# A transformer block with 32 routed experts: expert blocks 128 or 96 slots wide, and an adding DMA that skips empty slots

## The chip, the core and the metric

The kernel runs on one core of a Trainium2 chip. The metric is the device time of one execution in microseconds (us). A core has a matrix engine (PE, whose weight loads the profile lists apart as PEld), a vector engine (DVE), a scalar engine (ACT), a general engine (POOL) and a sync engine (SP), and 16 DMA engines that move data between the memory and the core's buffers.

## The reference, cut to what matters

The block takes 1024 tokens of width 1024. A dilated attention and a recurrent branch come first, then a projection, a norm and a router that gives every token the two best experts of one group of eight. The change lies in the last part, the experts:

```python
# per token: 2 experts of 32, each with a gate value
def expert_block(args):                       # xb: tokens of one expert, e: the expert
    xb, e = args
    hid = jax.nn.silu(xb @ w_expert_gate[e]) * (xb @ w_expert_up[e])   # 1024 -> 512
    return hid @ w_expert_down[e]                                      # 512 -> 1024
yb = lax.map(expert_block, (xin, blk_expert)).reshape(n_rows, D)
y = jax.ops.segment_sum(yb * row_gate[:, None], row_tok, num_segments=T + 1)[:T]
```

The result is added to the residual stream. All is float32. Weights are 6 MB an expert, 201 MB for the 32.

## The kernel before

Everything before 1159 us of the profile (projection, recurrent scan, attention, mixing, router) is the same in both kernels. From there the kernel runs one block per expert. A block has `CAP = 96` slots; an expert with more tokens has the rest done in a loop behind the blocks, which does not run for this data.

The token numbers of an expert stand in a column of the table `tbl`, one slot in a partition; a slot without a token holds a number past the last row (`1 << 20` and more). An indirect DMA from POOL (`gather`, L1504) brings the 96 rows into `xin`, a tile of 128 partitions by 1024; it has a bound, and rows past it are skipped, so that the 32 partitions above and the empty slots hold zeros or old rows.

float32 products are made of halves: each operand is split into a rounded part ("hi") and the rest ("lo"), and three matmuls stand for one: hi by hi, lo by hi, hi by lo. For the tokens, `xpose` transposes `xin` on PE (L1525, against `ident`) into a PSUM tile, four pieces at a time; ACT writes the hi half from it (L1526), DVE the lo half (L1527). The halves of the input are `xTh` and `xTl` (8 pieces, so two evictions each per expert), those of the hidden rows `hTh` and `hTl` (4 pieces, one each).

The weights of an expert come in 12 chunks of 512 KB (8 for gate and up, 4 for down) by SP's queue. Each is split: ACT makes hi (L1415), and lo is made by DVE for about ten chunks and by POOL for two (every sixth; the last 30 chunks all go to DVE), both L1417. The halves go into nine pairs of buffers `u`.

In `acc` (L1531) the token halves are stationary and 512 columns of the weights move. Gate and up are 48 matmuls into two PSUM tiles `pb`; ACT applies Silu to one (L1584), and DVE multiplies the other onto it (L1585), which gives `hd`. Down is 24 matmuls into two tiles `pa`, evicted with the gate value by DVE (L1605) and ACT (L1606) into `row`. Then `add_rows` (L1510) adds the rows to the output by an indirect DMA that POOL issues. It has no bound here: the output has 128 rows of padding, and the table `tba`, made by four small DVE instructions, points each empty slot at its own padding row.

The steps run (gate/up of expert e), (down of expert e-1), with the transposes of the next tokens and of the hidden rows put among the matmuls (`xpose_hi`). In which order each engine gets its instructions is decided when the program is built, by a scheduler that goes by its own estimate of each instruction's cost; `xpose_hi` gives the transposes and their evictions a higher priority.

Here a POOL or DVE "split" means the L1417 instruction (128x1024 in, 128x1024 out), "add" the instruction of L1510 and "gather" that of L1504.

Of the kernel before, what the change touches and what calls it, by code (L numbers as in the profile page):

```python
# [10 lines left out]
F32 = mybir.dt.float32  # L11
F32R = mybir.dt.float32r
BF = mybir.dt.bfloat16
I32 = mybir.dt.int32
U32 = mybir.dt.uint32
AF = mybir.ActivationFunctionType
ALU = mybir.AluOpType
# [4 lines left out]
S = 1024  # L22
# [16 lines left out]
CAP = 96  # L39
# [143 lines left out]
def block_kernel(ctx, tc, I, out, dbg=None):  # L183
    nc = tc.nc
# [31 lines left out]
    ident = cst.tile([128, 128], F32, name="ident")  # L216
# [64 lines left out]
    def pb(shape):  # L281
        return psB.tile([128] + shape, F32, name="pb")
# [38 lines left out]
    for k in range(8):  # L321
# [4 lines left out]
        if k == 7:  # L326
# [3 lines left out]
                                       op0=ALU.mult, op1=ALU.subtract)  # L330
        for i in range(2):
            for kk in ([k] if i == 0 or k > 1 else [] if k == 0 else [0, 1]):
                for h in range(2):
                    hs = slice(h * 512, (h + 1) * 512)
                    for n, (a, b) in enumerate(((0, xhi), (0, xlo), (1, xhi))):
                        nc.tensor.matmul(ps0[i][h], w0[i][a][:, kk, :], b[:, kk, hs],
                                         start=(kk == 0 and n == 0), stop=(kk == 7 and n == 2))
    for h in range(2):
        hs = slice(h * 512, (h + 1) * 512)
        for k in range(8):  # L340
            for n, (a, b) in enumerate(((0, xhi), (0, xlo), (1, xhi))):
                nc.tensor.matmul(ps0[2][h], w0[2][a][:, k, :], b[:, k, hs], start=(k == 0 and n == 0),
                                 stop=(k == 7 and n == 2))
# [12 lines left out]
    for h in range(2):  # L356
        pt = psB.tile([128, 4, 128], F32, name="pb")
# [52 lines left out]

# [1 line left out]
    hrs = [slice(0, 64), slice(64, 128)]  # L412
# [28 lines left out]
    pT = sT.enter_context(tc.tile_pool(name="pT", bufs=1, reuse_waits="tile"))  # L441
# [37 lines left out]
    for p in range(4):  # L479
        cs = slice(128 * p, 128 * p + 128)  # L480
        for h in range(2):
            hs = slice(h * 512, (h + 1) * 512)
            ps = pb([512])
# [6 lines left out]
            nc.gpsimd.dma_start(dGG[p][:, hs], gt)  # L490
# [1 line left out]
    tab = p1.tile([32, 12], F32, name="tab", bufs=1)  # L492
# [5 lines left out]
    for g in range(3):  # L498
        pt = psB.tile([128, 384], F32, name="pb")
# [45 lines left out]
    def prep(p):  # L545
# [18 lines left out]
        for h in range(2):  # L564
# [13 lines left out]
            for j in range(4):  # L578
                nc.tensor.matmul(pn[:, 2 * j:2 * j + 2], kks[:, j * 128:(j + 1) * 128], cc("ind2"),
                                 start=True, stop=True)  # L580
# [54 lines left out]
            tstep()  # L635
            # token-major copies
            BT = p1.tile([128, 4, 2, 128], F32, name="BT")
# [9 lines left out]
            tstep()  # L647
            # chunk-local products
            pbn = pb([512])
# [114 lines left out]
    if MP & 2 and not MP & 1:  # L764
        mp.enter_context(tc.manual_schedule(engines={mybir.EngineType.PE}))
# [1 line left out]
    s2 = ExitStack()  # L767
# [110 lines left out]

# [1 line left out]
    s3 = ExitStack()  # L880
# [211 lines left out]

# [1 line left out]
    pmx = s9.enter_context(tc.tile_pool(name="pmx", bufs=2, reuse_waits="tile"))  # L1094
# [57 lines left out]

# [1 line left out]
    def gate(gi, n, h, ga=None):  # L1154
# [62 lines left out]

# [1 line left out]
    def route(i, pl, r2):  # L1219
# [272 lines left out]
    rstep()  # L1492
    # slots without a token point past the last row
    gr = cst.tile([128, 64], F32, name="gr")
# [5 lines left out]

# [1 line left out]
    def gather(dst, src, idx):  # L1502
# [5 lines left out]
    def add_rows(src, idx):  # L1508
        src = src[0:idx.shape[0]]
        nc.gpsimd.indirect_dma_start(out=out, out_offset=bass.IndirectOffsetOnAxis(ap=idx, axis=0),  # L1510
                                     in_=src, in_offset=None, compute_op=ALU.add)

# [5 lines left out]
    def xpose(src, kt, name):  # L1518
        hi = pm.tile([128, kt, 128], F32R, name=name + "h")
        lo = pm.tile([128, kt, 128], F32R, name=name + "l")  # L1520
        sv = src.rearrange("q (p k) -> q k p", k=kt)
        for q in range(kt // 4):
            pt = pb([4, 128])
            for j in range(4):
                nc.tensor.transpose(pt[:, j], sv[:, 4 * q + j], ident)  # L1525
            nc.scalar.activation(hi[:, 4 * q:4 * q + 4], pt, AF.Copy)  # L1526
            nc.vector.tensor_tensor(lo[:, 4 * q:4 * q + 4], pt, hi[:, 4 * q:4 * q + 4].bitcast(F32), op=ALU.subtract)  # L1527
        return hi, lo

    def acc(ps, w, x, first, last):  # L1530
        nc.tensor.matmul(ps, x, w, start=first, stop=last)  # L1531

# [16 lines left out]
    tailm.close()  # L1549
    tpad = pm.tile([128, 2], F32, name="tpad")  # L1550
    nc.vector.tensor_scalar(tpad[:, 0:1], tokid[:, 0:1], float(S), None, op0=ALU.add)
    nc.vector.tensor_scalar(tpad[:, 1:2], tpad[:, 0:1], -1.0, float(1 << 20), op0=ALU.mult, op1=ALU.add)
    tba = pm.tile([128, 32], I32, name="tba")
    tocc = pm.tile([128, 32], F32, name="tocc")
    nc.vector.tensor_scalar(tocc, pT[:, 96:128], tpad[:, 1:2], tpad[:, 0:1], op0=ALU.mult, op1=ALU.add)
    nc.vector.tensor_tensor(tba, tocc, pT[:, 0:32], op=ALU.add)

# [4 lines left out]
    for m, e in steps:  # L1562
        if m == 0:
# [19 lines left out]
            hd = pm.tile([128, 512], F32, name="hd", bufs=2)  # L1583
            nc.scalar.activation(hd, pg_, AF.Silu, scale=rsl[:, e:e + 1])  # L1584
            nc.vector.scalar_tensor_tensor(hd, pu_, rsl[:, e:e + 1], hd, op0=ALU.mult, op1=ALU.mult)  # L1585
            hid[e] = hd
            if e == N_EXP - 1:
                hT = xpose_hi(hid.pop(e), 4, "hT")
        else:
# [14 lines left out]
            rw = row if e < N_EXP - 2 else xin[e % 2]  # L1604
            nc.vector.tensor_scalar(rw[:, 0:512], pd[0], gat[:, e:e + 1], None, op0=ALU.mult)  # L1605
            nc.scalar.activation(rw[:, 512:1024], pd[1], AF.Copy, scale=gat[:, e:e + 1])  # L1606
            add_rows(rw, tba[0:CAP, e:e + 1])
    s9.close()

    sm.close()  # L1610
# [1 line left out]
    dTBv = dTB.rearrange("(q e) w -> q e w", e=32)  # L1612
# [89 lines left out]
```

## Time and profile before

| what | us |
|---|---|
| median of three executions (1787.35, 1787.5, 1788.68) | 1787.5 |
| span of the profiled execution | 1787.2 |
| expert stage within it, from the first gate/up matmuls | 1159 to 1776 |
| busy over the whole span: PE, DVE, ACT, POOL | 1680.3, 1263.4, 873.7, 461.6 |

The span is the time between the first and the last instruction of the profiled execution; the execution's own time lies 0.3 us above it, which is the median. The busy share of PE over the whole says little on the expert stage, where DVE is busy nearly all the time; the stage has to be read by its own windows. In rows of the timeline the first number is the start, the second the duration, and a bracket gives the idle time before it and what ended that. A `x3` joins three neighbours into one row.

### The profile page before, as it was taken

How to read it: one execution, taken by the hardware profiler on the slowest of the kernel's cores; microseconds unless marked ns; L12 is line 12 of the kernel's file. 1: busy time of each engine (PE TensorE's matmuls, PEld its weight loads, DVE VectorE, ACT ScalarE, POOL GpSimd, SP SyncE). 2: the span in 40 equal slices, each digit the busy share in tenths (PEclk: the TensorE clock that was granted, in tenths of full speed). 3: DMA queues.
4: the chain of work that ended last, by engine and by line, in shares of the span. 5: the costliest groups of instructions: out<-in, count | busy, mean ns of one | idle time of the engine just before them, and what ended most of it. 6: DMA issues, size and time to landing. Idle time of an engine off the chain costs nothing. (4 is left out here: it accounts for less than half of the span.)

```text
span 1787.2 us, 25862 instructions
## 1 busy us (share of the span) xinstructions
PE 1680.3 (94%) x9395; PEld 1325.3 (74%) x9396; DVE 1263.4 (71%) x2122; ACT 873.7 (49%) x1315; POOL 461.6 (26%) x380
## 2 busy tenths in 40 slices
PE   8999999999999999999998999699998999899996
PEld 6677777777777777777766777588777877777884
DVE  5647788783664444444436666689999999999985
ACT  4523434422221333344342122388777888777774
POOL 0110112223431000000100311234455455444431
PEclk9998989998999999999999999799999999999998
DMA  8323223363662110111249773699999999999991
GB/s 285 138 69 133 92 92 116 136 241 119 219 198 80 33 45 30 48 40 51 101 145 259 220 288 130 220 307 362 358 349 309 378 343 382 356 354 360 373 348 28
DMA packets 145619, 363.44 MB, mean 203 GB/s; under 512 B 17316, under 2 KB 62772, under 8 KB 145484
## 3 DMA queue, kind: packets, MB, share of 16 engines
q1 hardware_dynamic: 123108, 303.67, 47.4%
q0 software_dynamic: 15872, 50.35, 10.1%
q10 hardware_dynamic: 6504, 7.69, 1.6%
q8 instruction: 76, 1.25, 0.3%
q14 instruction: 59, 0.48, 0.1%
HBM read 307.49 MB, written 62.29 MB: 207 GB/s over the span
## 5 line engine op out<-in xcount | busy, mean ns | idle before, releaser
L1531 PE MATMUL pb<-u,xTh 128*128 128x512 f32 x1024 | 338.4, 406 | 1.2 <-ACT xTh L1526 1.2
L307 PE MATMUL pa<-xlo,wh 128*128 128x512 f32 x736 | 307.7, 418 | 0.0
L307 PE MATMUL pa<-xhi,wl 128*128 128x512 f32 x736 | 302.1, 411 | 2.3 <-DVE wl L278 2.3
L307 PE MATMUL pa<-xhi,wh 128*128 128x512 f32 x736 | 301.7, 410 | 1.5 <-DVE raw L427 1.0
L1417 DVE TENSOR_TENSOR u<-raw,u 128x1024 fp32r<-128x1024 f32 x182 | 297.5, 1676 | 5.5 <-ACT u L1415 5.3
L1415 ACT ACTIVATE u<-raw 128x1024 fp32r<-128x1024 f32 x216 | 224.3, 1056 | 47.5 <-PE pb L1531 28.8
L1531 PE MATMUL pb<-u,xTl 128*128 128x512 f32 x512 | 209.2, 409 | 21.1 <-DVE xTl L1527 21.1
L1531 PEld LDWEIGHTS pb<-u,xTh 128*128 128x128 f32 x1024 | 191.3, 189 | 40.7 <-ACT xTh L1526 2.0
L307 PEld LDWEIGHTS pa<-xlo,wh 128*128 128x128 f32 x736 | 141.1, 192 | 40.6 <-issue 11.0
L307 PEld LDWEIGHTS pa<-xhi,wh 128*128 128x128 f32 x736 | 141.4, 192 | 34.5 <-issue 2.9
L307 PEld LDWEIGHTS pa<-xhi,wl 128*128 128x128 f32 x736 | 141.6, 192 | 34.1 <-DVE wl L278 3.2
L1417 DVE TENSOR_TENSOR u<-mix,u 128x1024 fp32r<-128x1024 f32 x108 | 162.2, 1538 | 4.4 <-ACT u L1415 4.4
L1531 PE MATMUL pa<-u,hTh 128*128 128x512 f32 x512 | 146.0, 406 | 5.5 <-POOL u L1417 4.6
L1415 ACT ACTIVATE u<-mix 128x1024 fp32r<-128x1024 f32 x128 | 133.6, 1057 | 23.1 <-PE pb L1531 15.8
L1531 PEld LDWEIGHTS pb<-u,xTl 128*128 128x128 f32 x512 | 96.8, 189 | 45.0 <-DVE xTl L1527 27.9
L978 DVE SCALAR_TENSOR_TENSOR Sb<-pb,rqk,bias 128x128 f32<-128x128 f32 (+1 forms) x96 | 35.5, 406 | 124.5 <-PE pb L977 116.6
L1510 POOL DMA_INDIRECT out<-row,tba x30 | 62.6, 2086 | 219.4 <-ACT u L1415 56.5
L1531 PEld LDWEIGHTS pa<-u,hTh 128*128 128x128 f32 x512 | 94.6, 191 | 28.2 <-POOL u L1417 5.5
L1417 POOL TENSOR_TENSOR u<-raw,u 128x1024 fp32r<-128x1024 f32 x34 | 101.3, 2980 | 47.2 <-ACT u L1415 41.6
L276 ACT ACTIVATE wh<-wr 128x1024 fp32r<-128x1024 f32 x49 | 51.8, 1057 | 113.9 <-PE pa L307 90.1
L1531 PE MATMUL pa<-u,hTl 128*128 128x512 f32 x256 | 81.6, 400 | 1.2 <-DVE hTl L1527 1.2
L982 ACT ACTIVATE Sb<-Sb,ML 128x128 f32<-128x128 f32 (+1 forms) x96 | 42.3, 442 | 54.7 <-DVE ML L980 54.7
(419 smaller groups left out, 3014.4 us busy)
## 6 DMA issues: line engine op xcount, KB each, us to landing
raw<-in_w_expert_up SPq DMA_DIRECT2D x72, 512.0 KB
raw<-in_w_expert_gate SPq DMA_DIRECT2D x71, 512.0 KB
raw<-in_w_expert_down SPq DMA_DIRECT2D x71, 512.0 KB
wr<-in_w_in SPq DMA_DIRECT2D x49, 512.0 KB
mix<-in_w_expert_down SPq DMA_DIRECT2D x46, 512.0 KB
mix<-in_w_expert_gate SPq DMA_DIRECT2D x42, 512.0 KB
mix<-in_w_expert_up SPq DMA_DIRECT2D x40, 512.0 KB
dGA<-gs POOLq DMA_DIRECT2D x32, 256.0 KB, 3.6
```

What stands on the lines that cost most here:

```text
L276: nc.scalar.activation(wh, wr, AF.Copy)
L307: nc.tensor.matmul(ps, a[:, k, :], b[:, k, hs], start=(n == 0), stop=(n == 23))
L978: nc.vector.scalar_tensor_tensor(Sb[:, hh, 0:nk], pS[:, 0:nk], u.rn[:, 0, i, hh:hh + 1], u.bias[:, hh, 256 - nk:], op0=ALU.mult, op1=ALU.add)
L982: nc.scalar.activation(Sb[:, hh, 0:nk], Sb[:, hh, 0:nk], AF.Exp, bias=u.ML[:, i, hh:hh + 1], accum_out=u.ML[:, i, 2 + hh:3 + hh])
L1415: nc.scalar.activation(hi, raw, AF.Copy)
L1417: en.tensor_tensor(lo, raw, hi.bitcast(F32), op=ALU.subtract)
L1510: nc.gpsimd.indirect_dma_start(out=out, out_offset=bass.IndirectOffsetOnAxis(ap=idx, axis=0), in_=src, in_offset=None, compute_op=ALU.add)
L1531: nc.tensor.matmul(ps, x, w, start=first, stop=last)
```

## The change

The expert blocks become 96 wide all through: the transposes take 96 rows and give 96 columns, the halves `xT` and `hT` are 8 and 4 pieces of 96 columns, the matmuls have 96 stationary columns and 96 result rows, and the evictions, Silu and the multiplication work on 96 partitions. The adding DMA takes `tbl` and a bound, as the gather does, so that empty slots are skipped; the four DVE instructions that made `tba` go. The padding rows of the output stay allocated, and nothing adds to them any more in the blocks.

```diff
     def add_rows(src, idx):
         src = src[0:idx.shape[0]]
         nc.gpsimd.indirect_dma_start(out=out, out_offset=bass.IndirectOffsetOnAxis(ap=idx, axis=0),
-                                     in_=src, in_offset=None, compute_op=ALU.add)
+                                     in_=src, in_offset=None, bounds_check=S - 1, oob_is_err=False, compute_op=ALU.add)
...
     def xpose(src, kt, name):
-        hi = pm.tile([128, kt, 128], F32R, name=name + "h")
-        lo = pm.tile([128, kt, 128], F32R, name=name + "l")
+        hi = pm.tile([128, kt, CAP], F32R, name=name + "h")
+        lo = pm.tile([128, kt, CAP], F32R, name=name + "l")
         sv = src.rearrange("q (p k) -> q k p", k=kt)
         for q in range(kt // 4):
-            pt = pb([4, 128])
+            pt = pb([4, CAP])
             for j in range(4):
-                nc.tensor.transpose(pt[:, j], sv[:, 4 * q + j], ident)
+                nc.tensor.transpose(pt[:, j], sv[0:CAP, 4 * q + j], ident[0:CAP, 0:CAP])
...
-        nc.tensor.matmul(ps, x, w, start=first, stop=last)
+        nc.tensor.matmul(ps[0:CAP], x, w, start=first, stop=last)
...
-    tpad = pm.tile([128, 2], F32, name="tpad")
-    nc.vector.tensor_scalar(tpad[:, 0:1], tokid[:, 0:1], float(S), None, op0=ALU.add)
-    nc.vector.tensor_scalar(tpad[:, 1:2], tpad[:, 0:1], -1.0, float(1 << 20), op0=ALU.mult, op1=ALU.add)
-    tba = pm.tile([128, 32], I32, name="tba")
-    tocc = pm.tile([128, 32], F32, name="tocc")
-    nc.vector.tensor_scalar(tocc, pT[:, 96:128], tpad[:, 1:2], tpad[:, 0:1], op0=ALU.mult, op1=ALU.add)
-    nc.vector.tensor_tensor(tba, tocc, pT[:, 0:32], op=ALU.add)
...
-            nc.scalar.activation(hd, pg_, AF.Silu, scale=rsl[:, e:e + 1])
-            nc.vector.scalar_tensor_tensor(hd, pu_, rsl[:, e:e + 1], hd, op0=ALU.mult, op1=ALU.mult)
+            hc, rc_ = hd[0:CAP], rsl[0:CAP, e:e + 1]
+            nc.scalar.activation(hc, pg_[0:CAP], AF.Silu, scale=rc_)
+            nc.vector.scalar_tensor_tensor(hc, pu_[0:CAP], rc_, hc, op0=ALU.mult, op1=ALU.mult)
...
-            nc.vector.tensor_scalar(rw[:, 0:512], pd[0], gat[:, e:e + 1], None, op0=ALU.mult)
-            nc.scalar.activation(rw[:, 512:1024], pd[1], AF.Copy, scale=gat[:, e:e + 1])
-            add_rows(rw, tba[0:CAP, e:e + 1])
+            gc = gat[0:CAP, e:e + 1]
+            nc.vector.tensor_scalar(rw[0:CAP, 0:512], pd[0][0:CAP], gc, None, op0=ALU.mult)
+            nc.scalar.activation(rw[0:CAP, 512:1024], pd[1][0:CAP], AF.Copy, scale=gc)
+            add_rows(rw, tbl[0:CAP, e:e + 1])
```

The changed sizes change the scheduler's estimates, and with them the order. Up to about the 18th expert every engine's order is the same as before; from there on it differs at several places.

POOL from the 18th add on, before (`row` is the evicted block, `u` a weight half, `xin` the gathered tokens):

```order
L1510 DMA out<-row,tba 1152x1024
L1417 TENSOR_TENSOR u<-mix,u 128x1024
L1417 TENSOR_TENSOR u<-raw_12892,u 128x1024
L1504 DMA xin_9920<-dH_77,tbl 96x1024
L1510 DMA out<-row,tba 1152x1024
```

The same place after the change:

```order
L1510 DMA out<-row,tbl 1152x1024
L1417 TENSOR_TENSOR u<-mix,u 128x1024
L1504 DMA xin_9920<-dH_77,tbl 96x1024
L1417 TENSOR_TENSOR u<-raw_12917,u 128x1024
L1510 DMA out<-row,tbl 1152x1024
```

The gather has moved from behind POOL's second split to ahead of it; between an add and the next there are still two splits and one gather.

DVE from the 21st `hd` on, before:

```order
L1585 SCALAR_TENSOR_TENSOR hd<-pb,gr,hd 128x512
L1527 TENSOR_TENSOR xTl<-pb,xTh 128x512
L1417 TENSOR_TENSOR u<-mix,u 128x1024
L1527 TENSOR_TENSOR xTl<-pb,xTh 128x512
L1417 TENSOR_TENSOR u<-mix,u 128x1024 x3
L1605 TENSOR_SCALAR row<-pa,gr 128x512
L1417 TENSOR_TENSOR u<-mix,u 128x1024
L1527 TENSOR_TENSOR hTl<-pb,hTh 128x512
```

The same place after:

```order
L1579 SCALAR_TENSOR_TENSOR hd<-pb,gr,hd 96x512
L1527 TENSOR_TENSOR xTl<-pb,xTh 128x384
L1417 TENSOR_TENSOR u<-mix,u 128x1024
L1600 TENSOR_SCALAR row<-pa,gr 96x512
L1417 TENSOR_TENSOR u<-mix,u 128x1024 x3
L1527 TENSOR_TENSOR hTl<-pb,hTh 128x384
```

The second `xTl` no longer stands behind `hd`: at these experts one of the two is made ahead of `hd`, between the splits. The multiplication and the row eviction have 96 partitions and the same 512 columns; the three lo evictions have 384 columns for 512.

PE at the end of an expert's gate/up part some experts later, just ahead of its first down matmuls (`pa`), before:

```order
L1531 MATMUL pb<-u,xTh 128x512
L1525 MATMUL pb<-ident,xin_9920 128x128
L1531 MATMUL pb<-u,xTl 128x512
L1525 MATMUL pb<-ident,xin_9920 128x128
L1531 MATMUL pb<-u,xTh 128x512
L1525 MATMUL pb<-ident,xin_9920 128x128
L1531 MATMUL pb<-u,xTh 128x512
L1531 MATMUL pb<-u,xTl 128x512
L1525 MATMUL pb<-ident,xin_9920 128x128 x4
L1531 MATMUL pa<-u,hTh 128x512 x4
```

The corresponding stretch after:

```order
L1531 MATMUL pb<-u,xTh 96x512
L1525 MATMUL pb<-ident,xin_9920 128x96 x4
L1531 MATMUL pb<-u,xTh 96x512
L1531 MATMUL pb<-u,xTl 96x512
L1531 MATMUL pb<-u,xTh 96x512 x2
L1531 MATMUL pb<-u,xTl 96x512
L1531 MATMUL pb<-u,xTh 96x512
L1525 MATMUL pb<-ident,xin_9920 128x96 x2
```

The eight transposes of the next tokens have moved from the very end of the gate/up part to its middle, in fours and twos; the number of matmuls is the same.

## The prediction, made before the changed kernel ran

> **What bounds the kernel now.** I read the page's busy rows and slices first, for where the changed part lies, then busy time by windows in the expert stage, then PE's own timeline and waits there, then one period of DVE and POOL. Of the page (the slices are fortieths of the span):
>
> ```profile
> span 1787.2 us, 25862 instructions
> PE 1680.3 (94%) x9395; PEld 1325.3 (74%) x9396; DVE 1263.4 (71%) x2122; ACT 873.7 (49%) x1315; POOL 461.6 (26%) x380
> DVE  5647788783664444444436666689999999999985
> ```
>
> DVE's 71% hides a stage: in the last third it is at nine tenths or more. Two windows of the expert stage (columns: window, length, PE, PEld, DVE, ACT, POOL busy, granted clock, DMA share, GB/s):
>
> ```profile
> 1284.88:1364.12 79.24, 73.07 (x336) 59.75 (x336) 79.24 (x62) 61.69 (x70) 37.31 (x16) 1.00 0.99 351
> 1651.10:1705.10 54.00, 54.00 (x256) 45.11 (x254) 49.70 (x44) 40.40 (x49) 26.98 (x12) 1.00 1.03 372
> ```
>
> In the first, four experts long, DVE has no idle moment and PE has; in the second, three experts, PE has none and DVE has. So the stage has two limits close together. PE's first down matmuls of some experts give their sizes:
>
> ```profile
> 1186.16 0.48 PE L1531 MATMUL pa<-u,hTh 128*128 128x512 f32 x1
> ...
> 1493.34 0.95 PE L1531 MATMUL pa<-u,hTh 128*128 128x512 f32 x3
> ...
> 1513.08 1.18 PE L1531 MATMUL pa<-u,hTh 128*128 128x512 f32 x4
> ...
> 1651.15 1.18 PE L1531 MATMUL pa<-u,hTh 128*128 128x512 f32 x4
> 1669.13 0.72 PE L1531 MATMUL pa<-u,hTh 128*128 128x512 f32 x2
> ...
> 1741.15 0.71 PE L1531 MATMUL pa<-u,hTh 128*128 128x512 f32 x2
> ```
>
> 1513.08 - 1493.34 = 19.74 us an expert where DVE sets the pace, 1669.13 - 1651.15 = 17.98 where PE does. From 1186.16 to 1741.15 there are 29 periods in 555.0 us; at 17.98 they would take 521.4. All that this change can give without making PE's own work shorter is thus 33.6 us. What PE waits for there:
>
> ```profile
> PE pb L1531 <- DVE xTl L1527: 21.1, 15, 1.6
> PE pa L1531 <- POOL u L1417: 4.6, 2, 2.8
> 1518.77 0.63 PE L1531 MATMUL pb<-u,xTh 128*128 128x512 f32 x2
> 1520.93 0.50 PE L1531 MATMUL pb<-u,xTl 128*128 128x512 f32 x1 [1.54 <-DVE xTl L1527]
> ```
>
> The 15 waits for the lo half of the tokens stand once per slow expert. DVE is late as a whole, and this is where PE finds out. One DVE period, from one `hd` to the next, and POOL beside it:
>
> ```profile
> 1499.72 0.74 DVE L1585 SCALAR_TENSOR_TENSOR hd<-pb,gr,hd 128x512 f32<-128x512 f32 x1
> 1500.39 0.67 DVE L1527 TENSOR_TENSOR xTl<-pb,xTh 128x512 fp32r<-128x512 f32 x1
> ...
> 1506.12 0.73 DVE L1605 TENSOR_SCALAR row<-pa,gr 128x512 f32<-128x512 f32 x1
> 1506.78 1.21 DVE L1417 TENSOR_TENSOR u<-raw,u 128x1024 fp32r<-128x1024 f32 x1
> 1507.92 0.67 DVE L1527 TENSOR_TENSOR hTl<-pb,hTh 128x512 fp32r<-128x512 f32 x1
> 1508.52 4.34 DVE L1417 TENSOR_TENSOR u<-raw,u 128x1024 fp32r<-128x1024 f32 x1
> 1512.78 4.57 DVE L1417 TENSOR_TENSOR u<-raw,u 128x1024 fp32r<-128x1024 f32 x2
> ...
> 1519.54 0.74 DVE L1585 SCALAR_TENSOR_TENSOR hd<-pb,gr,hd 128x512 f32<-128x512 f32 x1
> 1507.66 1.66 POOL L1510 DMA_INDIRECT out<-row,tba  x1 [9.26 <-DMA mxh<-in_w_expert_down]
> 1508.85 2.92 POOL L1417 TENSOR_TENSOR u<-raw,u 128x1024 fp32r<-128x1024 f32 x1
> 1512.85 3.42 POOL L1417 TENSOR_TENSOR u<-mix,u 128x1024 fp32r<-128x1024 f32 x1 [1.08 <-ACT u L1415]
> ```
>
> Start to start, a split that nothing holds up costs 1.13 (1506.78 to 1507.92), an eviction 0.60 (1507.92 to 1508.52), `hd` and `row` 0.66 each (1506.12 to 1506.78). By the code ten splits, three lo evictions and the two others stand in a period: 11.35 + 1.80 + 1.33 = 14.48. The period is 19.82. The missing 5.34 stands in two splits: the one at 1508.52 takes 4.26 until the next start instead of 1.13 (3.13 more), and among the two at 1512.78 one has 3.43 instead of 1.21 (2.22 more). Both run while POOL runs a split of its own, and each ends 1.09 after POOL's does (1512.86 against 1511.77). DVE therefore stands still behind POOL's splits for over a quarter of the period.
>
> **The narrower lo evictions.** DVE's time goes by columns. Two rows that differ in columns only:
>
> ```profile
> L1225 DVE SCALAR_TENSOR_TENSOR lg<-pb,r,br x8: 240/242/244, 1038.8 to 1143.2; 128x32 f32<-128x32 f32 x8
> L1527 DVE TENSOR_TENSOR hTl<-pb,hTh x32: 672/676/692, 1177.7 to 1769.3; 128x512 fp32r<-128x512 f32 x32
> ```
>
> (676 - 242) / 480 = 0.904 ns a column, so 384 columns for 512 save 0.115 us an eviction, 0.345 an expert. `hd` and `row` keep 512 columns and lose only partitions: nothing. How much of the 0.345 counts? `hTl` stands just ahead of the first blocked split. That split's end hangs on POOL's, and POOL's on the add, which is issued on `row`, before `hTl`. So a shorter `hTl` only makes the split begin to wait earlier: I count 0.23, with 0.345 as the other end. In the first 19 experts the order is unchanged, and PE stands 19 x 0.23 = 4.4 us less (6.6 at the other end).
>
> **The new order from expert 19.** Before, an add is followed by two splits of POOL and then the gather; now by a split, the gather, a split. The trace has this order already in its fast stretch:
>
> ```profile
> 1654.01 2.42 POOL L1417 TENSOR_TENSOR u<-raw,u 128x1024 fp32r<-128x1024 f32 x1 [1.05 <-ACT u L1415]
> 1654.41 3.11 DVE L1417 TENSOR_TENSOR u<-raw,u 128x1024 fp32r<-128x1024 f32 x1
> 1657.44 0.68 DVE L1527 TENSOR_TENSOR xTl<-pb,xTh 128x512 fp32r<-128x512 f32 x1
> 1662.70 4.56 DVE L1417 TENSOR_TENSOR u<-raw,u 128x1024 fp32r<-128x1024 f32 x2
> 1667.19 3.48 DVE L1417 TENSOR_TENSOR u<-mix,u 128x1024 fp32r<-128x1024 f32 x3
> ```
>
> There the blocked splits lose 3.03 - 1.13 = 1.90 and 4.49 - 2.27 = 2.22, together 4.12 for 5.34, since POOL's split no longer stands in line behind the add's descriptors. With the 0.345, DVE's sum becomes 14.48 - 0.345 + 4.12 = 18.25. Experts 19 to 23 took 98.4 us before (19.8 each, the last 19.1); at 18.25 they take 91.3: 7.1 less. The second `xTl` that now comes ahead of `hd` moves no work, it only makes the wait at 1520.93 come later, on `hd` or a split; I give it nothing. Experts 24 to 28 already stand on PE's 17.98: nothing.
>
> **PE.** 72 matmuls and 12 transposes an expert stay. The matmuls move 512 columns as before; I take 17.98 as it is. The weight loads get narrower, 96 columns for 128, but they lie under the matmuls:
>
> ```profile
> L1531 PEld LDWEIGHTS pb<-u,xTh x1024: 186/188/333, 1159.0 to 1765.4; 128*128 128x128 f32 x171
> L1003 PEld LDWEIGHTS pb<-PT,Vt x280: 132/136/138, 600.4 to 919.8; 128*64 128x64 f32 x140
> ```
>
> By these, 96 columns take about 162 ns, 26 less than 188, under a matmul step of 230 ns (the rows of the first down matmuls: three take 0.95, four 1.18). Between nothing and 72 x 0.026 = 1.9 us an expert I take nothing, the row of the fast window being PE busy without a gap. The Trainium skill, "TensorE: Matmul & The Clock Gate", section "LDWEIGHTS (loading the stationary operand)", has the load grow with the columns at P / 1.2 ns, 107 for 128, and the trace has 188; by its slope the same 27 ns would go, so the sum would not differ by it.
>
> **The add.** Its DMA traffic falls: empty slots move nothing. That traffic is on no path: SP's loads wait for buffers, not the engines for loads.
>
> ```profile
> SPq L1320 <- DVE u L1417: 195.0, 175, 3.4
> L1510 POOL DMA_INDIRECT out<-row,tba x30: 1637/1660/6590, 1194.9 to 1749.1; - x30
> L1504 POOL DMA_INDIRECT xin<-dH,tbl x32: 965/1802/1902, 1149.8 to 1705.6; - x32
> ```
>
> No loads come sooner for it, since what a load waits for is the split that frees `raw`. The bound could change the add's time on POOL. The nearest row is the gather, which has a bound and as many rows: 0.965 at least, 1.802 in the middle, against 1.637 and 1.660. An add that lets POOL's split begin sooner or later moves DVE by as much, so the ends are -0.67 and +0.14 an expert, over some 24 experts -16 and +3.4. I take nothing: it is the same instruction on the same 96 slots, and the gather's two durations differ by what DVE does beside it, not by the bound. The longest add, 6.59, is a stray one; PE's two waits for POOL's split, 4.6 together, are what such an add leaves behind. It may come or go, and is kept.
>
> **Start and tail.** The four small DVE instructions go (about 0.1 to 0.2 us each, beside the first matmuls), the first and last evictions are shorter and stand on the path: together I put 0.5, an estimate.
>
> Sum: -4.4 - 7.1 - 0.5 = -12.0 on the profiled execution's 1787.2, with 0.3 around it (it stands at the median, 1787.5): **1775.5 us**.
>
> **Rivals.**
> (a) *DVE slips in front of POOL.* Which of the two splits holds the other hangs on a few tenths: DVE's split starts 0.33 ahead of POOL's (1508.52 against 1508.85) and is blocked all the same. With `hTl` 0.115 shorter it starts 0.45 ahead. If that is enough to keep it running, only POOL's later work meets DVE: a period of 14.48 - 0.345 + 2.22 + 1.90 (POOL's delayed split against the next of DVE's, taken as in the fast stretch) = 18.25 from the start. Over some 24 slow experts 24 x 0.27 = 6.5 of the 33.6 us stay: 1760, and 1754 if nothing stays. Against it: the start, 1508.52, lies inside the add (1507.66 to 1509.32), and 0.115 sooner still does; it would have to slip in ahead of what the add leaves for POOL to do, not of the split alone.
> (b) *Nothing is passed on.* Each blocked split is tied to POOL, so shorter evictions before either of the two are eaten, the new order loses to new collisions or to a stray add of 6.6 us more: 1785, between 1781 and 1789.
> (c) *96 is another geometry (slower).* PE changes between the transposes, which have 96 rows, and the matmuls, with 96 columns:
>
> ```profile
> 437.81 0.86 PE L865 MATMUL pb<-UVs,MCs 128*64 128x64 f32 x12
> 438.60 0.50 PE L307 MATMUL pa<-xlo,wh 128*128 128x512 f32 x1
> ```
>
> In the first row 12 matmuls take 0.06 apart and the next geometry begins about 0.15 after the last: 0.09 us a change. With some 16 changes an expert, 1.4 us, PE's floor becomes 19.4, and 31 experts take about 1793. It decides from 0.1 us a change on, where PE overtakes DVE's 19.6. The Trainium skill, "TensorEngine Tiling (Array Packing)", section "Key Properties", says that changing the tiling mode drains the engine; its section "Tiling Modes" knows 128, 64 and 32 only, by which 96 stays in the full array and costs nothing. No run here shows 96.
> (d) *The load counts.* If the matmul step does follow the load, PE's floor falls by up to 1.9 us. That is seen only where DVE has time left, 49.70 of 54.00 for three experts, so 1.4 us for each of the last five: 7 more, 1768.
>
> **Chances.** My forecast 0.52, with a range of its own of 1768 to 1782 (an add shorter by half of 0.67 in the first 19; nothing from the new order); (a) 0.20; (b) 0.16; (c) 0.07; (d) 0.05. The range from 1755 to 1788 takes in (a) but for its best end, (d), and (b) but for its worst end, and leaves out (c): under 2 in 10 together. A measurement of this kernel tells 0.2%, 3.6 us, from no change: faster takes the forecast, (a), (d) and a little of (b), 0.80; same is most of (b), 0.12; slower is (c) and the worst of (b), 0.08.
>
> **What would show it.** Right: in the profile after, the lo evictions of L1527 at 0.56 us; PE at 17.98 in the fast stretch; the period of the early experts near 19.6 with both blocked splits still there; experts 19 to 23 near 18.3; PE's waits for `xTl` down from 21.1 to some 10. Wrong: a period near 18.2 from the start (a); `xTl` waits unchanged (b); PE's fast stretch longer than 17.98 (c) or shorter (d); an add that is not 1.66.

## The result, and the profile after

The changed kernel took 1768.2 us, median of 11 executions (1752.47 to 1776.86), against 1788.68 for the kernel before (11 executions, 1778.11 to 1801.95): a ratio of 0.9871, 95% interval 0.9842 to 0.9899. The forecast was 1775.5. The profiled execution is one of the quickest, 1754.57 with a span of 1752.7:

```profile
span 1752.7 us, 25894 instructions
PE 1662.1 (95%) x9395; PEld 1253.9 (72%) x9396; DVE 1208.9 (69%) x2118; ACT 853.5 (49%) x1315; POOL 504.3 (29%) x380
```

The two spans can't be set against each other as they stand. In all profiles of this study the work ahead of the expert stage ended anywhere from 1142.8 to 1172.6 us, though its instructions are the same but for a few that zero a tile in some of the runs. One such place, before and then after (the column behind the brackets is the granted clock):

```profile
400.00:430.00 30.00, 28.38 (x360) 22.93 (x359) 11.19 (x21) 7.45 (x12) 9.98 (x16) 0.72 0.31 103
```

```profile
400.00:430.00 30.00, 27.44 (x470) 21.99 (x468) 11.15 (x21) 9.81 (x17) 12.22 (x20) 1.00 0.36 115
```

In the execution with the lower clock, 360 matmuls ran in these 30 us where the other ran 470. So I compare the expert stage alone, from its first gate/up matmul to the end, and split it at the first down matmuls of the experts, which PE's timeline shows. For the changed kernel:

```profile
1172.82 0.68 PE L1531 MATMUL pa<-u,hTh 128*96 128x512 f32 x2
...
1512.89 0.68 PE L1531 MATMUL pa<-u,hTh 128*96 128x512 f32 x2
...
1605.41 0.40 PE L1531 MATMUL pa<-u,hTh 128*96 128x512 f32 x1
...
1706.62 0.64 PE L1531 MATMUL pa<-u,hTh 128*96 128x512 f32 x2
```

Their distances, worked out in the same way for all kernels (us; "start" is the first gate/up matmul, "stage" runs from there to the end of the span; 29 experts lie between the first and the last boundary):

| kernel | start | experts 0-18 | 19-23 | 24-28 | stage |
|---|---|---|---|---|---|
| before | 1159.0 | 366.6 | 98.4 | 90.0 | 628.3 |
| the change | 1146.4 | 340.1 | 92.5 | 101.2 | 606.3 |
| hTl_in_two | 1158.1 | 341.6 | 92.4 | 101.2 | 608.3 |
| hTl_narrow_alone | 1149.9 | 365.7 | 98.5 | 89.7 | 629.6 |
| bound_alone | 1152.3 | 367.3 | 98.4 | 89.6 | 627.4 |
| bound_and_hTl | 1168.3 | 368.1 | 98.4 | 89.4 | 629.7 |
| no_bound | 1172.6 | 340.2 | 92.4 | 101.1 | 608.3 |
| strided_96 | 1156.6 | 343.8 | 95.2 | 101.5 | 614.5 |
| tokens_side_96 | 1167.6 | 361.0 | 97.2 | 103.1 | 635.0 |
| hidden_side_96 | 1158.0 | 360.5 | 92.3 | 97.7 | 624.8 |
| no_late_pool | 1156.7 | 340.2 | 91.1 | 93.7 | 598.8 |
| before_no_pool | 1153.5 | 341.6 | 89.9 | 89.9 | 595.1 |
| after_no_pool | 1169.3 | 339.6 | 89.5 | 94.1 | 595.4 |
| order_held_no_pool | 1142.8 | 339.5 | 89.2 | 97.1 | 596.3 |

The stage fell by 22.0 us, close to the 20.5 of the medians. It did so by two things of opposite sign: 26.5 us less in the first 19 experts and 5.9 in the next five, then 11.2 us *more* in 24 to 28. The kernel before was not slow throughout its first 19 experts: ten of their periods are 19.7 to 20.0 us, one is 23.9, and eight are 18.0 to 18.5. At 17.98 each the 19 would have taken 341.6, so 25.0 of the 26.5 us are DVE no longer being late, and 1.5 are PE's own pace, which is 17.8 to 18.0 in this execution. In the first stretch, nineteen experts, PE has no gap left; in the last it has (windows of the changed kernel):

```profile
1172.80:1512.90 340.10, 340.10 (x1600) 248.88 (x1598) 332.75 (x284) 278.52 (x323) 227.72 (x76) 1.00 1.00 361
1605.40:1706.60 101.20, 92.01 (x421) 64.28 (x420) 82.52 (x76) 69.86 (x86) 33.97 (x17) 1.00 1.01 369
```

PE's waits for DVE's `xTl`, 21.1 us before, are gone, and its waits for POOL's splits have risen from 4.6:

```profile
PE pb L1531 <- POOL u L1417: 6.2, 6, 1.1
PE pa L1531 <- POOL u L1417: 5.2, 6, 1.0
```

How DVE got faster in the first stretch, two experts of it (rows of DVE, then of POOL):

```profile
1291.42 0.54 DVE L1527 TENSOR_TENSOR hTl<-pb,hTh 128x384 fp32r<-128x384 f32 x1
1291.89 5.75 DVE L1417 TENSOR_TENSOR u<-raw,u 128x1024 fp32r<-128x1024 f32 x5
1297.96 0.75 DVE L1579 SCALAR_TENSOR_TENSOR hd<-pb,gr,hd 96x512 f32<-96x512 f32 x1 [0.33 <-PE pb L1531]
...
1308.33 0.54 DVE L1527 TENSOR_TENSOR hTl<-pb,hTh 128x384 fp32r<-128x384 f32 x1
1308.80 10.57 DVE L1417 TENSOR_TENSOR u<-mix,u 128x1024 fp32r<-128x1024 f32 x5
1319.30 0.74 DVE L1579 SCALAR_TENSOR_TENSOR hd<-pb,gr,hd 96x512 f32<-96x512 f32 x1
```

```profile
1291.17 1.96 POOL L1510 DMA_INDIRECT out<-row,tbl  x1 [6.72 <-DMA mix<-in_w_expert_up]
1292.65 10.61 POOL L1417 TENSOR_TENSOR u<-raw,u 128x1024 fp32r<-128x1024 f32 x2
1303.39 1.82 POOL L1504 DMA_INDIRECT xin<-dH,tbl  x1
1308.08 4.39 POOL L1510 DMA_INDIRECT out<-row,tbl  x1 [2.87 <-DMA raw<-in_w_expert_down]
1311.99 2.93 POOL L1417 TENSOR_TENSOR u<-mix,u 128x1024 fp32r<-128x1024 f32 x1
1315.88 2.41 POOL L1417 TENSOR_TENSOR u<-mxh,u 128x1024 fp32r<-128x1024 f32 x1 [0.96 <-PE pb L1531]
```

In the first of the two, five DVE splits follow one another undisturbed (5.75), and it is POOL's pair that stands still (10.61). DVE even runs into a wait of its own (0.33). In the second, POOL gets its turn and DVE's five splits take 10.57. The periods from `hd` to `hd` alternate so, 14.5 and 21.3, where the slow experts of the kernel before had 19.8. Their mean, 17.9, is PE's own pace. DVE still stands still here: what its splits take above 1.21 us each is 3.5 us an expert over the first 19, where it was 4.9 before.

### The profile page after: what moved, and what is told of

The parts are those of the page before. It is cut to its first block, busy times and chain, and to the rows that moved or that the text cites. A ratio compares the mean times of both kernels' runs of the same rounds, so it can differ in the third digit from the quotient of the medians.

```text
span 1752.7 us, 25894 instructions
## 1 busy us (share of the span) xinstructions
PE 1662.1 (95%) x9395; PEld 1253.9 (72%) x9396; DVE 1208.9 (69%) x2118; ACT 853.5 (49%) x1315; POOL 504.3 (29%) x380
## 5 line engine op out<-in xcount | busy, mean ns | idle before, releaser
L1531 PE MATMUL pb<-u,xTh 128*96 128x512 f32 x1024 | 340.8, 406 | 7.2 <-POOL u L1417 6.2
L1417 DVE TENSOR_TENSOR u<-raw,u 128x1024 fp32r<-128x1024 f32 x182 | 248.8, 1408 | 15.5 <-ACT u L1415 15.0
L1415 ACT ACTIVATE u<-raw 128x1024 fp32r<-128x1024 f32 x216 | 221.7, 1055 | 28.5 <-PE pb L1531 17.9
L1531 PEld LDWEIGHTS pb<-u,xTh 128*96 128x96 f32 x1024 | 165.2, 164 | 73.7 <-POOL u L1417 9.0
L1531 PE MATMUL pb<-u,xTl 128*96 128x512 f32 x512 | 204.0, 399 | 0.0
L1531 PE MATMUL pa<-u,hTh 128*96 128x512 f32 x512 | 143.4, 399 | 6.0 <-POOL u L1417 5.2
L1417 POOL TENSOR_TENSOR u<-raw,u 128x1024 fp32r<-128x1024 f32 x34 | 132.5, 3904 | 48.1 <-ACT u L1415 27.4
L1510 POOL DMA_INDIRECT out<-row,tbl x30 | 77.5, 2584 | 147.6 <-ACT row L1601 36.9
L1531 PEld LDWEIGHTS pa<-u,hTh 128*96 128x96 f32 x512 | 80.1, 163 | 42.3 <-POOL u L1417 10.0
L1531 PEld LDWEIGHTS pb<-u,xTl 128*96 128x96 f32 x512 | 83.2, 163 | 30.7
L1531 PE MATMUL pa<-u,hTl 128*96 128x512 f32 x256 | 80.1, 394 | 0.9 <-DVE hTl L1527 0.9
```

What stands on the lines that cost most here:

```text
L1415: nc.scalar.activation(hi, raw, AF.Copy)
L1417: en.tensor_tensor(lo, raw, hi.bitcast(F32), op=ALU.subtract)
L1531: nc.tensor.matmul(ps[0:CAP], x, w, start=first, stop=last)
```

## The experiments

**1. Is it the eviction next to the add?** My theory T: `hTl`, 0.13 us shorter, lets the split behind it start sooner against the add, and that settles which engine gets ahead. Two runs: one makes the eviction in two pieces inside the change, so that it is longer again; the other shortens it alone in the kernel before, where its rows then have gaps (96 of every 128 columns).

```diff
-            nc.vector.tensor_tensor(lo[:, 4 * q:4 * q + 4], pt, hi[...], op=ALU.subtract)
+            for a, b in ((0, 4),) if name == "xT" else ((0, 2), (2, 4)):
+                nc.vector.tensor_tensor(lo[:, 4 * q + a:4 * q + b], pt[:, a:b], hi[...], op=ALU.subtract)
```

> The changed kernel, with the lo eviction of the hidden rows made by two DVE instructions of 192 columns in place of one of 384. By the rows the second instruction adds about 0.14 us, so this eviction lasts as long as the 128-wide one did (0.62 against 0.60), while all else of the change stays; every engine's order stays that of the changed kernel but for a few rows in the last two experts. Theory T (the start of the split behind this eviction against POOL's add decides who gets ahead): that split starts again about 0.85 us after the add, POOL's two splits hold DVE up again, the experts 4 to 18 take 19.6 us each, and the expert stage loses some 22 us of its gain: ratio to the kernel before about 1.00, 19.6 in the periods. Rival W (it is DVE's work: 0.345 us less an expert, or the bound): 0.14 us an expert come back at most, periods stay 17.9, ratio 0.987 to 0.990.

Measured: 0.986 (0.981 to 0.991), 1765.4 us; the first 19 experts take 341.6, near the 340.1 of the change. The split behind the eviction starts 0.79 us after the add, about half way from the change's 0.72 to the 0.86 of the kernel before, and runs through. T's forecast of a return to 19.6 fails.

```diff
+            n = CAP if name == "hT" else 128
-            nc.vector.tensor_tensor(lo[:, 4 * q:4 * q + 4], pt, hi[...], op=ALU.subtract)
+            nc.vector.tensor_tensor(lo[:, 4 * q:4 * q + 4, 0:n], pt[:, :, 0:n], hi[..., 0:n], op=ALU.subtract)
```

> The kernel before, with the lo eviction of the hidden rows alone narrowed to 96 of 128 columns in each piece (the other columns of that tile are zeroed once at the start, by four DVE instructions); matmuls, transposes, the other evictions, the add without a bound and each engine's order stay as before but for a few rows at the start. Theory T: this one instruction of 0.12 us less an expert is enough: the split behind it starts 0.73 us after the add, DVE stays ahead, experts 4 to 23 take about 18 us where they took 19.8, up to 33 us less in all, and the last experts don't lose since their order is the old one: ratio 0.981 to 0.985. Rival W: 0.12 us an expert, at most 3 us in all, ratio 0.998 to 1.000, periods 19.7.

Measured: 1.002 (0.998 to 1.006), 365.7 in the first 19. T fails here too. One expert of it, DVE and then POOL (line numbers are each kernel's own):

```profile
1285.35 0.54 DVE L1531 TENSOR_TENSOR hTl<-pb,hTh 128x384 fp32r<-128x384 f32 x1
1285.82 5.60 DVE L1417 TENSOR_TENSOR u<-mix,u 128x1024 fp32r<-128x1024 f32 x2
```

```profile
1285.09 1.66 POOL L1510 DMA_INDIRECT out<-row,tba  x1 [9.26 <-issue]
1286.28 2.91 POOL L1417 TENSOR_TENSOR u<-mix,u 128x1024 fp32r<-128x1024 f32 x1
```

The split starts 0.73 us after the add (1285.82 against 1285.09) and is held; in the change it starts 0.72 after (1291.89 against 1291.17) and runs through. The start alone does not decide.

**2. Is it the bound?** Three runs: the bound alone in the kernel before (the four small DVE instructions go with it); the change without it; and bound and narrowed `hTl` together in the kernel before.

```diff
-                                     in_=src, in_offset=None, compute_op=ALU.add)
+                                     in_=src, in_offset=None, bounds_check=S - 1, oob_is_err=False, compute_op=ALU.add)
...
-            add_rows(rw, tba[0:CAP, e:e + 1])
+            add_rows(rw, tbl[0:CAP, e:e + 1])
```

> The kernel before, with the add's table and bound of the change (empty slots skipped, the four small DVE instructions gone), all widths 128 and every order as before. Theory T: the add on POOL is as long as it was, 1.66 us, nothing moves: ratio 0.998 to 1.002, periods 19.8. Rival B (the bound shortens the add or the traffic, and that lets DVE ahead): periods near 18, ratio 0.98 to 0.99.

Measured: 0.9972 (0.9938 to 1.0005); 367.3 in the first 19, stage 627.4. The add and its collisions stay; what is left of the ratio lies within the interval.

The change with the old table and no bound (these two lines as before, and the four small DVE instructions back):

> The changed kernel with the add of before: table tba, made by the four small DVE instructions, and no bound; widths 96 and every engine's order those of the changed kernel. Theory TB (two things together let DVE ahead: the split behind the hidden rows' eviction starts no later than about 0.8 us after the add, and the add has the bound and takes the port later): the split at 0.72 us is held as it was with the eviction narrowed alone, periods near 19.6, ratio 0.995 to 1.002. Rival W (the widths do it, by all three lo evictions together): periods 17.9, ratio 0.986 to 0.989.

Measured: 0.9877 (0.9828 to 0.9926), 340.2, 92.4 and 101.1, row by row the change. The adding DMA's bound takes no part in the result.

The edits of hTl_narrow_alone and bound_alone together:

> The kernel before with the bound on the add and the hidden rows' lo eviction of 96 columns, the two that did nothing alone; the other evictions 128 wide, order as before but for a few rows at the start. Theory TB: DVE gets ahead, periods near 18 up to the last experts, which keep their 17.9: ratio 0.980 to 0.985. Rival W: periods 19.7, ratio 0.997 to 1.001.

Measured: 0.9977 (0.9951 to 1.0003), 368.1. TB fails; the widths do it. That `hTl` takes no part is not shown: here, too, it was narrowed with gaps, and in one piece it was never narrowed alone.

**3. Which of the widths?** The tiles' layout, then each side of the block by itself.

```diff
-        hi = pm.tile([128, kt, CAP], F32R, name=name + "h")
+        hi = pm.tile([128, kt, 128], F32R, name=name + "h")[:, :, 0:CAP]
```

(and `lo` likewise)

> The changed kernel, with the halves of 96 columns kept in tiles of 128 columns a piece, so that the evictions write and read rows of 4 x 96 with gaps (as in the run that narrowed the hidden rows' eviction alone) in place of 384 in one piece; widths and every order as in the changed kernel. Theory S (it is the form of the eviction in one piece that lets DVE ahead): periods 19.6, ratio 0.997 to 1.002. Rival W (the widths, by DVE's shorter work): periods 17.9 up to the 21st expert, ratio 0.985 to 0.989.

Measured: 0.994 (0.991 to 0.997), 343.8 in the first 19, with two experts of 19.4 and 19.0 among them and the rest at 17.96 to 18.03. That is neither value that was expected. DVE also gets ahead with gaps in the rows, but not each time, as the count below shows, so the form is not the whole cause and is not without effect.

The kernel before with one side 96 wide (`W` is 96 for the side named, else 128):

```diff
+        W = CAP if name == "xT" else 128
-        hi = pm.tile([128, kt, 128], F32R, name=name + "h")
+        hi = pm.tile([128, kt, W], F32R, name=name + "h")
...
-            pt = pb([4, 128])
+            pt = pb([4, W])
-                nc.tensor.transpose(pt[:, j], sv[:, 4 * q + j], ident)
+                nc.tensor.transpose(pt[:, j], sv[0:W, 4 * q + j], ident[0:W, 0:W])
...
```

> The kernel before with the tokens' side alone 96 wide: transposes, both evictions of xT, the gate and up matmuls, Silu and the multiplication; the hidden rows' side stays 128 wide (the rest of hd is zeroed once), the add has its old table and no bound. The order is that of before up to the 21st expert, and the splits' lead falls from the 22nd on. Theory W (DVE's shorter work): of the 0.345 us an expert 0.23 go here, DVE gets ahead from the third expert on, early periods 18; with the late loss the ratio is 0.985 to 0.990. Theory H (the hidden rows' side, which stands next to the add, is needed): early periods 19.6, ratio 0.998 to 1.003.

Measured: 1.001 (0.997 to 1.004); 361.0 in the first 19 and 103.1 in the last five.

> The kernel before with the hidden rows' side alone 96 wide: their transposes, both evictions in one piece of 384, the down matmuls and the row evictions on 96 partitions; the tokens' side stays 128 wide, the add has its old table and no bound. The order is that of before up to the 22nd expert. Theory W: 0.115 us an expert are too little, early periods 19.7, ratio 0.998 to 1.004 with the late loss. Theory H: early periods 18, ratio 0.984 to 0.990.

Measured: 0.9975 (0.9948 to 1.0001); 360.5. Neither W's 366 nor H's 341 in either of the two. What PE waits for in the run of the hidden side, and its adds:

```profile
PE pa L1532 <- POOL u L1417: 20.8, 20, 1.9
```

```profile
L1510 POOL DMA_INDIRECT out<-row,tba x30: 1641/7796/7804, 1194.1 to 1745.9; - x30
```

This is a third pattern. From the third add to the 20th DVE wins each time, the add takes 7.80 us for 1.66 (16 of the 30), POOL's splits behind it come late, and PE waits for those, 1.0 us twenty times. So DVE ahead is not good by itself. The two sides alone save 5.6 and 6.1 us in the first 19 experts and both together 26.5: together they happen to give the alternation in which PE waits for nobody.

The run of the tokens' side shows both outcomes in one kernel. DVE and POOL at two successive adds:

```profile
1396.62 4.33 DVE L1417 TENSOR_TENSOR u<-raw,u 128x1024 fp32r<-128x1024 f32 x1
1416.17 1.21 DVE L1417 TENSOR_TENSOR u<-mix,u 128x1024 fp32r<-128x1024 f32 x1
```

```profile
1395.77 1.66 POOL L1510 DMA_INDIRECT out<-row,tba  x1 [4.46 <-ACT u L1415]
1415.31 7.93 POOL L1510 DMA_INDIRECT out<-row,tba  x1 [7.85 <-ACT u L1415]
```

The split starts 0.85 and 0.86 us after the add; the first is held, the second is not. Counted over the 13 adds from the third to the 17th that stand ahead of `hTl` (the tenth and the 14th stand behind it), the split behind `hTl` ran through (1.2 us, not held):

| kernel | `hTl` | ran through, of 13 |
|---|---|---|
| before, bound_alone | 512 columns | 0 |
| hTl_narrow_alone, bound_and_hTl | 384, with gaps | 0 |
| tokens_side_96 | 512 columns | 4 |
| strided_96 | 384, with gaps | 8 |
| the change, no_bound, hidden_side_96 | 384, in one piece | 13 |
| no_late_pool | 384, in one piece | 12 |
| hTl_in_two | 2 x 192, in one piece | 13 |

Every kernel with the hidden rows' halves 96 wide and in one piece has DVE ahead at 12 or all of the 13. Gaps on both sides take it down to 8 (strided_96), so the form has a part in it; which else on that side (the matmuls, the row evictions) no run separates.

**4. Is it POOL's splits at all?** If they are what the stage loses by, the kernel before, still 128 wide, must gain by giving them to DVE.

```diff
-PTL = 30
+PTL = 400
```

> The kernel before, 128 wide and without the bound, but POOL splits no weight chunk in the whole expert stage: all lo halves are DVE's. ACT's and PE's order as before but for a few rows at the start. Theory P (what bounds the stage is DVE standing still behind POOL's splits, not DVE's own work): DVE's sum is 12 x 1.135 + 3 x 0.60 + 2 x 0.66 = 16.7 us an expert, under PE's 17.9, so all experts run at 17.9 to 18.0: some 30 us less, ratio 0.981 to 0.985. Rival Q (two more splits an expert make DVE the later one: POOL's adds and gathers, which starve when DVE's instructions stand back to back, come late): periods of 19 or more, ratio 0.995 or above.

Measured: 0.9776 (0.9732 to 0.9821), 1749.2 us, below the change. PE in 20 experts:

```profile
1180.00:1539.00 359.00, 359.00 (x1678) 300.04 (x1677) 340.96 (x340) 304.71 (x340) 77.39 (x40) 1.00 1.03 371
```

PE is busy without a gap, and all 29 periods are 17.98 or 17.99. The stage takes 595.1 us, 33.2 less than before: nearly all of the 33.6 that the prediction counted as the most that can be had at PE's pace. DVE makes 12 splits for 10 and is busy 340.96 / 20 = 17.0 us an expert, where with ten it took 19.8 in the slow experts, standing still included.

> The changed kernel with all lo halves of the expert stage made by DVE; ACT's order that of the changed kernel, with the short lead in the last experts. Theory P (the change's gain is nothing but who stands behind whom at POOL's splits): with those gone the 96 wide kernel is no faster than the 128 wide one without them: experts 0 to 21 take 17.87 for 17.98 (2.5 us less), the last six 18.7 for 17.98 (5 more): an expert stage of 596 to 599 us against 595, ratio 0.977 to 0.981. Rival W (the narrower evictions are worth time of their own): the stage falls by some 10 us more, ratio 0.971 to 0.974.

Measured (the same line in the changed kernel): 0.9796 (0.9757 to 0.9836), 1753.2 us, stage 595.4 against 595.1. Theory P holds: with POOL's splits gone, the 96 wide kernel is no faster than the 128 wide one. It is 2.4 us faster in the first 24 experts (17.84 to 17.99 a period for 17.98) and 4.2 slower in the next five, where its order has the shorter lead (part 5).

**5. The late loss.** In the built order I count how many chunks ACT has split ahead of the Silu of each expert, less 12 for every expert before it: 11 in both kernels up to the 18th (counted from 0); in the change this lead then falls by one an expert, to 5 at the 24th, and in the kernel before it does so five experts later. The lead alone is not the loss: at leads of 7 and 6 the kernel before takes 17.98 and 18.08 us (experts 27 and 28, where POOL makes hardly any split any more), the change 19.1 and 19.8 (22 and 23). In the change, PE, ACT and POOL in one of these experts:

```profile
1628.92 0.71 PE L1531 MATMUL pa<-u,hTh 128*96 128x512 f32 x2 [0.99 <-POOL u L1417]
...
1639.03 0.47 PE L1531 MATMUL pb<-u,xTh 128*96 128x512 f32 x1 [1.04 <-POOL u L1417]
```

```profile
1624.73 0.68 ACT L1578 ACTIVATE hd<-pb,gr 96x512 f32<-96x512 f32 x1 [4.05 <-PE pb L1531]
1625.31 1.04 ACT L1415 ACTIVATE u<-raw 128x1024 fp32r<-128x1024 f32 x1
```

```profile
1626.50 2.37 POOL L1417 TENSOR_TENSOR u<-raw,u 128x1024 fp32r<-128x1024 f32 x1 [2.68 <-issue]
```

ACT stands 4.05 us before Silu while hi halves wait behind it; the hi half made next ends at 1626.35, POOL's lo half of it at 1628.87, and PE goes on at 1628.92. On DVE the same step would be shorter:

```diff
-PTL = 30
+PTL = 90
```

> The changed kernel, with the last 90 weight chunks' lo halves all made by DVE (before: the last 30), so that POOL makes no split in the experts 24 to 28; every other order stays. Theory L (those experts take 20.5 us since POOL's split of a chunk whose hi half ACT makes only after Silu comes too late for PE): a DVE split takes 1.2 us for POOL's 2.4, the two waits of about 1.0 and 1.4 us an expert go, periods 18 to 18.5, some 11 us less than the changed kernel: ratio to before 0.980 to 0.983. Rival D (the splits' shorter lead in the order is the loss, whoever makes them): periods stay 20 or more, ratio 0.986 to 0.989.

Measured: 0.985 (0.979 to 0.990), 1762.3 us. Experts 24 to 28 take 93.7 for 101.2, 18.75 each for 20.5; 7.5 of the 11.2 us come back. L is right for the larger part; the ratio, beyond the band expected, carries the first part's uncertainty, the stage (598.8) is plain.

Last, ACT, DVE and POOL held to the written order over the whole loop, which keeps the lead at 11 chunks:

```diff
+    manx.enter_context(tc.manual_schedule(engines={ACT, DVE, POOL}))
     for m, e in steps:
```

> The changed kernel with all lo halves made by DVE, and with ACT, DVE and POOL held to the order in which the program is written through the expert stage, so that the splits keep their lead (11 chunks at each Silu, where the scheduler's order lets it fall to 5 from the 20th expert on). Theory L (the short lead is what costs the last experts the rest): 17.9 in all periods, no rise at the end: 14 us below the changed kernel, ratio 0.978 to 0.981. Rival M (the written order puts evictions behind splits that are not ready, and PE waits for them): periods above 18.3 throughout, ratio 0.985 or above.

Measured: 0.9779 (0.9742 to 0.9816), 1751.6 us. Up to the 25th expert all periods are 17.83 to 17.90, where after_no_pool, with the short lead, has 18.75 in the 24th and 25th: the lead's part, 0.9 us an expert. But 26 to 28 took 19.6, 22.3 and 19.5. One add there lasted 16.19 us, between DVE instructions that stand back to back, and `row`, which has one buffer, was taken so long. So this run bears L out for two experts only and gives no net gain.

## Why the prediction came out right, by its own steps

**The total** lay in the range, 1768.2 against 1775.5, but by luck more than by its steps. The first 19 experts gave 22.1 us more than forecast, and experts 24 to 28 cost 11.2 us where nothing was forecast; the two misses have opposite signs. The case that came was not the one I held likeliest.

**The lo evictions**, forecast at 0.56 us, took 0.544 (the two rows that gave 0.904 ns a column differ in the operation too; between this row and the 0.676 of before it is 1.03), and the weight loads 161 ns:

```profile
L1527 DVE TENSOR_TENSOR xTl<-pb,xTh x64: 540/544/553, 1147.2 to 1710.3; 128x384 fp32r<-128x384 f32 x64
L1531 PEld LDWEIGHTS pb<-u,xTh x1024: 159/161/284, 1146.4 to 1730.7; 128*96 128x96 f32 x171
```

The step for the evictions is right in its size and wrong in what it was taken to do. It was sized as work taken from a busy engine, 0.23 an expert, 4.4 us in the first 19, though only the ten slow ones among them could pass it on. Measured: 26.5. The step that failed is the rule "shorter work on the late engine shortens the period by as much". DVE's period holds 5.3 us that are not work but standing still, and these follow from a pattern, not from a sum. Rival (a), DVE ahead of POOL, is what happened, with a chance of 0.20. Its period (18.25 from the start) was near the 17.9 found, and its total, 1760, lacks the late loss. Its cause, a start 0.115 us sooner, does not hold: splits were held at 0.73 and 0.85 us after the add and ran through at 0.72, 0.79 and 0.86.

**The new order in experts 19 to 23**, 7.1 us, against 5.9 measured. The amount is near by two more misses that cancel: 19 to 21 run at 17.9 where 18.25 was forecast, and the loss of the last experts already begins in 22 and 23 (19.1 and 19.8). That the moved gather gave any of it is not shown.

**"Experts 24 to 28 already stand on PE's 17.98: nothing."** This failed by 11.2 us. I looked for what the new order moves on POOL and DVE and took PE's and ACT's for neutral. The lead of the splits over Silu, which the order shows without any trace, I did not count.

**The add**, forecast as unchanged, is unchanged by its bound (bound_alone, no_bound). Its time rose in the change, to a median of 1.96, by what DVE does beside it. The add of 6.59 was no stray one: in the kernel before, with the bound or a narrower `hTl` or both added, and with either side alone 96 wide, the tenth and the 14th add take 6.3 to 6.6 us; in the change they take 3.05 and 2.94. These are the two that start 1.1 to 1.2 us behind `hTl`, not ahead of it.

**PE's floor**: mostly 17.84 to 17.90 in the change, 17.98 before. I gave it nothing; bound_alone, 128 wide, has 17.88 and tokens_side_96 has 18.05, so the tenth can't be put down to the width. No step became shorter by the narrower loads beyond that, which leaves rivals (c) and (d) without support; with (c) the period would have been 19.4. The Trainium skill, "TensorEngine Tiling (Array Packing)", section "Tiling Modes", lists 128, 64 and 32; by that, 96 is no mode of its own, and the trace agrees: 17.84 to 17.90 us an expert with 96-row transposes among the matmuls.

**DMA** is off the path, as forecast: no wait of PE names a weight load in the stage.

What stays open: what decides at each add which of the two engines wins. The same start (0.72 to 0.73 us after the add) was held in one kernel and ran through in another, and 0.85 to 0.86 did both in one kernel. The Trainium skill, "SBUF — State Buffer", section "SBUF: two separate sides", gives the port that the two share to whichever instruction starts first, for its whole length. By that rule the held split of experiment 1, which starts 0.46 us ahead of POOL's split (1285.82 against 1286.28), can only be held by the add ahead of both; but then the same add should hold the split of the changed kernel, and it does not. So the rule by itself does not tell the two runs apart.

## What to carry to other kernels

Two engines that hold each other up can settle into a pattern, and an edit of a few tenths of a microsecond an expert moved this kernel from one pattern to another, worth six times the 4.4 us forecast for the work saved. Then ask what the collision costs at all, and try to take it away: here two fewer instructions an expert on the "helping" engine gave 2.2% by themselves, more than the whole change's 1.3%, and left the change worth nothing. Where a scheduler sets the order, count in the built order how far each producer runs ahead of its user: a fall in that lead can foretell a wait that no trace of before shows.

## What the runs showed of the hardware that was not expected

- A POOL instruction can starve behind DVE's. An indirect DMA's issue that takes 1.45 us at the least took 7.80 in 16 of 30 cases of one kernel (hidden_side_96), and 16.19 once in another (order_held_no_pool), between DVE instructions standing back to back:

```profile
L1510 POOL DMA_INDIRECT out<-row,tbl x30: 1448/2424/16193, 1177.6 to 1705.2; - x30
```

The Trainium skill, "SBUF — State Buffer", section "Who interferes with whom", infers that a `tensor_tensor` of DVE leaves the generation of DMA descriptors alone. Here the whole issue of an indirect DMA stood still while DVE made hardly anything but `tensor_tensor`; which access of the issue was held these rows don't show, so they neither bear the inference out nor refute it.

- The loser is not always the same: at starts within 0.01 us of each other DVE's split was held for 3.3 us in one kernel (hTl_narrow_alone) and not at all in another (the change), each time over many experts, and in tokens_side_96 the two outcomes stand side by side.
- The part of the program that no kernel changed took from 1142.8 to 1172.6 us, with granted clocks of 0.72 and 1.00 at one place, while the expert stage of kernels alike agreed within 2.3 us (before, bound_alone, bound_and_hTl and hTl_narrow_alone: 627.4 to 629.7). Comparing stages told apart what the medians could not.
